# The mLSTM's running maximum spread over the partitions and masked by GpSimd instead of by TensorE products

## The chip, the core and the metric

One NeuronCore of a Trainium2 chip runs the whole program in one launch. The metric is device time in microseconds (us), the median over executions. PE is TensorE, ACT ScalarE, DVE VectorE, POOL GpSimd, SP the queue that issues the weight loads.

## What is computed

Two layers, each an FFN, a mixing sub-layer of three branches (stick-breaking attention, mLSTM, latent attention) and another FFN, over 256 tokens of width 1024. The change lies in the mLSTM branch: four heads of 128, chunks of 128, started from a zero state. Per head:

```python
cum_f = jnp.einsum('bhs,ts->bht', lfc, lower_incl)
log_intra = jnp.where(causal, cum_f[..., :, None] - cum_f[..., None, :] + igc[..., None, :], -jnp.inf)
log_inter = cum_f + m_prev[..., None]
m = jnp.maximum(log_inter, jnp.max(log_intra, axis=-1))
w_intra = jnp.exp(log_intra - m[..., None])
scores = jnp.einsum('bhtd,bhsd->bhts', qc, kc) * w_intra
num = scores @ vc + w_inter[..., None] * (qc @ c_prev)
h_out = num / jnp.maximum(jnp.abs(den), jnp.exp(-m))[..., None]
```

The kernel treats both chunks at once. With g = ig - cum and mx the running maximum of g (not below 0), the weight of key s for query t is exp(g[s] - mx[t]) for s <= t, otherwise 0. Keys lie on the partitions, so g is a bias per partition, while mx, a row over the queries, has to be spread over all 128 partitions.

## The kernel before

The program is written out ahead of time by a planner in the kernel itself. The main line is a list of units, each some TensorE products with a weight tile; weights come from memory as fp32 (`raw`), ScalarE rounds them to a high part (`whi`, or `g` where a larger buffer is used), VectorE subtracts to get the low part (`wlo<-raw,whi`, a subtraction of two SBUF tiles of 128x1024), and three products make one of full precision. All else (norms, attention heads, mLSTM heads) runs as side work: Python generators that name, at each `yield`, the engine they go to next, the tiles they read and the buffers they need. Between units the planner lets every side go on whose inputs it reckons ready by costs of its own (`Flow.cost`, which charges a POOL instruction other than tensor_tensor 60 ns and 0.8 ns a column), and so fixes the order of each engine's queue. Each engine then runs its queue strictly in that order, and waits where an input isn't there.

The mLSTM is in two of these. `ml_side` transposes the gates to rows, scans them to `cum` and `mx`, and lays the gate columns `gcol` out by partitions. It had each row twice (8 rows), to hold mx as a high and a low part in a tile `mv` (tag R3). `ml_head`, once per head, spread mx with a product of the constant `sel` and `mv` into PSUM (`pd`), added the mask with two bf16 products, and took the scores in another (`pS`). Then ScalarE's exponential with bias g, VectorE's multiply with the scores, TensorE's product with the values (129 columns: the last one sums), and a normalisation: squares on ScalarE, six small vector instructions, a reciprocal root on POOL (`rstd`: an add and a power), and two output rows `xn` on VectorE. `y_t` transposes the output for two heads at a time.

In names of the profile and of the order, digits behind a letter are left out: `t` is the scratch tag t384 with six buffers (t_2 is t384_2), `at` a PSUM bank, `R` one of R1 (convolved q and k), R3 or R4, `consts_bf` the bf16 identity and masks, `qk` the stick-breaking pair's q and k. All instructions of the helpers carry the helper's line, L213 before and L210 in the changed kernel, so they are told by tiles.

Of the kernel before, what the change touches and what calls it, by code (L numbers as in the profile page):

```python
# [24 lines left out]
BIG = 1e30  # L25
# [4 lines left out]
NSMALL = GATES - MLI  # L30
R_SB, R_ML, R_GATE, R_CONVW, R_CONVB, R_QN, R_KVN, R_G1, R_G2, R_G3, N_ROWS = (
    0, 4, 12, 36, 68, 76, 78, 79, 87, 95, 103)
C_ID, C_TRI, C_ONES, C_INVF, C_MSB, C_MML, C_MLA, C_SEL, C_ROW, C_END = (
    0, 128, 256, 384, 416, 544, 672, 800, 1312, 1316)

LN128 = float(np.float32(128.0 ** -0.5))
RS128 = float(np.float32(128.0 ** -0.5))
# [4 lines left out]
def host_consts():  # L42
    c = np.zeros((P, C_END), np.float32)
    i = np.arange(P)
    row, col = i[:, None], i[None, :]
    c[:, C_ID:C_ID + P] = np.eye(P, dtype=np.float32)
    c[:, C_TRI:C_TRI + P] = np.where(row >= col, -1.0, 0.0)
    c[:, C_ONES:C_ONES + P] = -1.0
    c[:, C_MSB:C_MSB + P] = np.where(row >= col, -BIG, 0.0)
    c[:, C_MML:C_MML + P] = np.where(row > col, BIG, 0.0)  # L50
    c[:, C_MLA:C_MLA + P] = np.where(col > row, -BIG, 0.0)
    f = np.power(np.float32(10000.0), -np.arange(16, dtype=np.float32) / np.float32(16)).astype(np.float32)
    c[:, C_INVF:C_INVF + 16] = f
    c[:, C_INVF + 16:C_INVF + 32] = f
    for h in range(4):
        c[[h, h + 4], C_SEL + h * P:C_SEL + (h + 1) * P] = 1.0
    c[0:8, C_ROW:C_END] = [[1, 0, float(r >= 4), 1 - 2 * float(r >= 4)] for r in range(8)]
    return c


# [166 lines left out]
class Trunk:  # L227
# [248 lines left out]
    def setup(self, N):  # L476
        nc, a = self.nc, self.a
        self.c = self.const([P, C_MSB], "consts")
        self.xg = self.const([P, 8 + 8 * S], "x")
        self.x = self.xg[:, 8:].rearrange("p (k c) -> p k c", k=8)  # L480
        self.sel = self.const([P, 4, P], "sel", F32R)
        self.ident = self.c[:, C_ID:C_ID + P]
        self.tri = self.const([P, P], "tri", F32R)
        self.nones = self.c[:, C_ONES:C_ONES + P]
        self.ones_r = self.const([P, P], "ones_r", F32R)
        self.cb = self.const([P, 4, P], "consts_bf", BF16)
        self.ident_bf = self.cb[:, 0, :]
        self.mask_sb, self.mask_ml, self.mask_mla = (self.cb[:, i, :] for i in (1, 2, 3))
        self.mhalf = self.const([P, 16], "mhalf")
        self.row = self.const([8, 4], "row")  # L490
# [46 lines left out]
    def setup_late(self):  # L537
        nc, a = self.nc, self.a
        nc.sync.dma_start(self.c[:, C_TRI:C_ONES], a["consts"][:, C_TRI:C_ONES])
        nc.sync.dma_start(self.c[:, C_INVF:], a["consts"][:, C_INVF:C_MSB])  # L540
        sel = self.sb([P, 4, P], "qk96", 2)
        nc.sync.dma_start(sel, a["consts"][:, C_SEL:C_ROW].rearrange("p (h c) -> p h c", h=4))
        nc.sync.dma_start(self.row, a["consts"][0:8, C_ROW:C_END])
        msk = self.t384([P, 3, P])
        nc.sync.dma_start(msk, a["consts"][:, C_MSB:C_SEL].rearrange("p (m c) -> p m c", m=3))
# [5 lines left out]
        nc.vector.tensor_copy(self.cb[:, 1:4, :], msk)  # L551
        self.give(msk)
        nc.vector.tensor_copy(self.sel, sel)
        nc.vector.tensor_copy(self.tri, self.c[:, C_TRI:C_TRI + P])
        posf = self.sb([P, 2], "posf")
        nc.vector.tensor_copy(posf, pos)
# [27 lines left out]
        m = 1.5 * 2.0 ** 23  # L584
# [389 lines left out]
    def plan_mix(self, l, U, M, N):  # L974
        nc, a = self.nc, self.a
# [8 lines left out]
        def first_side():  # L984
            yield lambda: "row" in U,
            M["small"] = self.sb([P, 2, NSMALL], "small")
            M["sbv"] = self.sb([P, 2, 256], "sbv")
            M["ifg"] = self.sb([P, 2, 2, 2, 4], "ifg")
            M["done"] = set()
            M["mla"] = {}  # L990
            for t in range(2):
                yield "v", box[0][:, t], U["r"]
                r = U["r"][:, t:t + 1]
                nc.vector.scalar_tensor_tensor(M["small"][:, t], box[0][:, t, :NSMALL], r, M["bias1"][:, :NSMALL], ALU.mult, ALU.add)
                nc.vector.tensor_copy(M["ifg"][:, t], M["small"][:, t, 0:8].rearrange("p (g h) -> p g h", g=2).unsqueeze(2).to_broadcast([P, 2, 2, 4]))
# [423 lines left out]
    def ml_side(self, M):  # L1419
        nc = self.nc  # L1420
        small = M["small"]
        gates = M["ifg"].rearrange("p t g d h -> p t g (d h)")
        yield "p", small, ("ps", 1), (lambda: self.exp_ready(M))
        pt = self.ps()
        for t in range(2):
            for g in range(2):
                nc.tensor.transpose(pt[0:8, g * S + t * P:g * S + (t + 1) * P], gates[:, t, g], self.ident)
        rows = self.sb([8, 3, S], "R4")
        e, cum, g = rows[:, 0], rows[:, 1], rows[:, 2]
        mv = self.sb([P, S + P], "R3", dt=F32R)  # L1430
# [7 lines left out]
        nc.vector.scalar_tensor_tensor(e, pt[0:8, S:], 0.0, e, ALU.min, ALU.subtract)  # L1438
        nc.vector.tensor_tensor_scan(cum, one.to_broadcast([8, S]), e, 0.0, ALU.mult, ALU.add)
        nc.vector.tensor_tensor(g, pt[0:8, :S], cum, ALU.subtract)  # L1440
        self.give(pt)
        yield "v",
        mx, e = e, cum
        nc.vector.tensor_tensor_scan(mx, zero.to_broadcast([8, S]), g, 0.0, ALU.add, ALU.max)
        nc.vector.tensor_tensor(e, cum, mx, ALU.add)
        yield "a", e
        nc.scalar.activation(e, e, AF.Exp, scale=-1.0)

        nc.vector.tensor_copy(mv[0:8, 0:S], mx)
        nc.vector.tensor_scalar(mx, mx, low, None, ALU.mult)  # L1450
        nc.vector.scalar_tensor_tensor(mv[0:8, 0:S], mv[0:8, 0:S].bitcast(F32), sign, mx, ALU.mult, ALU.add)
        nc.vector.tensor_copy(mv[0:8, S:], mv[0:8, P:S].bitcast(F32))
        yield "p", e, ("ps", 1)
        pc = self.ps()
        for t in range(2):
# [14 lines left out]
    def ml_head(self, h, M, B):  # L1470
# [1 line left out]
        mm = nc.tensor.matmul  # L1472
        mx, gc, y = B["mx"], B["gc"], B["y"]
        qk, v, og = M["mlqk"], M["mlv"], M["og"]
        yield "p", mx, ("ps", 2), ("t384", 1)
        pd, pS, w = self.ps(), self.ps(), self.t384()
        mm(pd[:, 0:384], lhsT=self.sel[:, h, :], rhs=mx, start=True, stop=False, skip_group_check=True)
        for o in (0, 256):
            mm(pd[:, o:o + 128], lhsT=self.ident_bf, rhs=self.mask_ml, start=False, stop=True, skip_group_check=True)
        mm(pS[:, 0:256], lhsT=qk[:, 4 + h, 0:128], rhs=qk[:, h, :], start=True, stop=True)  # L1480
        mm(pS[:, 256:384], lhsT=qk[:, 4 + h, 128:256], rhs=qk[:, h, 128:256], start=True, stop=True)
        yield "a", pd[:, :384]
        for s, sl in ((0, slice(0, 256)), (1, slice(256, 384))):
# [110 lines left out]
```

## Time and profile before

| | |
|---|---|
| Time, median of 3 (lowest to highest) | 810.89 us (810.3 to 811.42) |
| Profiled execution, its time | 811.12 us |
| Its span | 809.1 us |
| Mean granted TensorE clock | 0.999 of full |
| TensorE busy | 801.9 us (99%) |
| VectorE, ScalarE busy | 611.8 us (76%), 472.3 us (58%) |
| POOL busy | 33.2 us (4%), 50 instructions |

The span runs from the first to the last instruction; the time also holds some 2 us around it. TensorE's busy time counts products that overlap, so lengths of steps are read from start to start. Busy shares say where the work is; what a change is worth shows in who waits for whom.

### The profile page before, as it was taken

Reading aid. Unit: us, or ns where it says so; the run is one execution under the profiler, and the core shown is the slowest. Engines: PE = TensorE matmul, PEld = TensorE weight load, DVE = VectorE, ACT = ScalarE, POOL = GpSimd, SP = SyncE. Lnnn points to the kernel's source line nnn. Section 1 sums busy time; section 2 is a strip of 40 time slices with the busy share of each in tenths; the row PEclk is TensorE's granted clock in tenths of the full one; section 3 lists DMA queues with packets and bytes.
Section 4 is the critical chain, followed back from the end, with each engine's and each line's share of the span. In section 5 each row is a group of like instructions: output and inputs, shape, how many; then the busy total and the mean of one; then the engine's idle time right before and its main releaser. Section 6 shows DMA issues by size and latency. Waiting matters only on the chain.

```text
span 809.1 us, 14902 instructions
## 1 busy us (share of the span) xinstructions
PE 801.9 (99%) x5927; PEld 756.6 (94%) x5927; DVE 611.8 (76%) x1023; ACT 472.3 (58%) x776; POOL 33.2 (4%) x50
## 2 busy tenths in 40 slices
PE   8999999999999999999999999999999999999998
PEld 6999999899999999889988899998999999988887
DVE  4888878987766588986787768789977585888851
ACT  5656545657686546765556555565567845657530
POOL 0000001200200000000000000110002000000000
PEclk9999999999999999999999999999999999999999
DMA  8767744653344745775576656266553555476721
GB/s 260 235 199 252 254 131 122 220 176 116 105 153 162 254 164 199 238 239 184 152 233 206 182 170 195 74 191 187 157 158 98 180 187 188 160 223 220 236 73 52
DMA packets 43844, 145.30 MB, mean 180 GB/s; under 512 B 6016, under 2 KB 7296, under 8 KB 43776
## 3 DMA queue, kind: packets, MB, share of 16 engines
q1 hardware_dynamic: 43632, 144.10, 56.3%
q8 instruction: 46, 0.75, 0.4%
q10 hardware_dynamic: 144, 0.27, 0.1%
q14 instruction: 22, 0.18, 0.1%
HBM read 143.30 MB, written 1.05 MB: 178 GB/s over the span
## 4 chain that ended last, share of the span: by engine, by line
PE 97%; DMA 1%; DVE 0%; ACT 0%; SPq 0%; issue 0%; ACTq 0%; DVEq 0%
PE mm L213 66%; PE at L213 31%; DMA raw<-in_weights_dram 1%; SPq L213 0%; DVE t L213 0%; ACT g L213 0%; DVE hs L213 0%; ACT s2k L213 0%; DVE g L213 0%; DVE u L213 0%; DVE xn L213 0%; ACT u L213 0%; ACTq L213 0%; DVEq L213 0%
## 5 line engine op out<-in xcount | busy, mean ns | idle before, releaser
L213 PE MATMUL mm<-u,whi 128*128 128x256 f32 (+1 forms) x1432 | 299.4, 300 | 0.0
L213 ACT CAST whi<-raw 128x1024 fp32r<-128x1024 f32 (+3 forms) x184 | 187.9, 1032 | 132.5 <-DMA raw<-in_weights_dram 54.9
L213 DVE TENSOR_TENSOR wlo<-raw,whi 128x1024 fp32r<-128x1024 f32 (+3 forms) x184 | 218.1, 1195 | 43.2 <-ACT whi L213 42.4
L213 PEld LDWEIGHTS mm<-u,whi 128*128 128x128 f32 x1432 | 227.1, 188 | 10.8 <-issue 0.5
L213 PE MATMUL mm<-u,wlo 128*128 128x256 f32 x840 | 234.2, 279 | 0.0
L213 PE MATMUL mm<-u,g 128*128 128x512 f32 (+1 forms) x992 | 156.5, 316 | 2.5 <-ACT g L213 2.1
L213 PEld LDWEIGHTS mm<-u,wlo 128*128 128x128 f32 x840 | 157.7, 188 | 0.0
L213 PEld LDWEIGHTS mm<-u,g 128*128 128x128 f32 x992 | 139.4, 192 | 15.5 <-ACT g L213 3.0
L213 ACT CAST g<-raw 128x1024 fp32r<-128x1024 f32 (+3 forms) x89 | 90.0, 1014 | 76.1 <-DMA raw<-in_weights_dram 45.3
L213 DVE TENSOR_TENSOR g<-raw,g 128x1024 fp32r<-128x1024 f32 (+3 forms) x89 | 104.2, 1178 | 13.0 <-ACT g L213 12.7
L213 PE MATMUL at<-R,whi 128*128 128x256 f32 x416 | 73.4, 278 | 0.0
L213 PE MATMUL at<-R,g 128*128 128x256 f32 x552 | 66.4, 279 | 0.0
L213 PEld LDWEIGHTS at<-R,g 128*128 128x128 f32 x552 | 65.2, 188 | 0.0
L213 PEld LDWEIGHTS at<-R,whi 128*128 128x128 f32 x416 | 63.3, 187 | 0.1
L213 PE MATMUL at<-R,wlo 128*128 128x256 f32 x208 | 57.8, 278 | 0.0
L213 PE MATMUL mm<-whi,u 128*128 128x512 f32 (+1 forms) x168 | 55.0, 384 | 0.0
L213 PEld LDWEIGHTS at<-R,wlo 128*128 128x128 f32 x208 | 39.0, 187 | 0.0
L213 DVE TENSOR_TENSOR R<-s2k,R 128x256 fp32r<-128x256 f32 (+1 forms) x39 | 17.9, 458 | 26.3 <-ACT R L213 26.0
L213 PEld LDWEIGHTS mm<-whi,u 128*128 128x128 f32 x168 | 31.6, 188 | 5.0
L213 PE MATMUL mm<-wlo,u 128*128 128x512 f32 (+1 forms) x84 | 32.1, 382 | 0.0
L213 DVE TENSOR_TENSOR s2k<-s2k,mm 128x512 f32<-128x512 f32 x38 | 26.0, 683 | 2.9 <-ACT s2k L213 2.5
L213 POOL TENSOR_TENSOR rcol<-rcol,mhalf 128x2 f32<-128x2 f32 x6 | 7.8, 1298 | 488.2 <-DVE rcol L213 488.2
(214 smaller groups left out, 984.8 us busy)
## 6 DMA issues: line engine op xcount, KB each, us to landing
raw<-in_weights_dram SPq DMA_DIRECT2D x245, 512.0 KB, 4.3
raw<-in_weights_dram SPq DMA_DIRECT2D x14, 384.0 KB, 3.5
raw<-in_weights_dram SPq DMA_DIRECT2D x8, 424.0 KB, 3.6
raw<-in_weights_dram SPq DMA_DIRECT2D x6, 256.0 KB, 4.5
bc<-in_b_in_dram SPq DMA_DIRECT2D x2, 512.0 KB, 4.6
x<-in_x_dram SPq DMA_DIRECT2D x3, 256.0 KB, 6.5
out_dram<-xn SPq DMA_DIRECT2D x3, 256.0 KB, 2.1
mg<-in_ml_out_norm_dram SPq DMA_DIRECT2D x2, 256.0 KB, 4.9
```

What stands on the lines that cost most here:

```text
L213: f(*args, **kw)
```

## The change

The row mx is no longer spread and masked by TensorE. Four small copies through SP put the four rows at partitions 0, 32, 64 and 96 of `mv`. In each head POOL spreads its row over 128 partitions (`partition_broadcast`) into the scratch tile `w`; ScalarE takes the exponential there, and POOL then sets the entries above the diagonal to zero (`affine_select`, twice per head). The constants `sel` and the mask of the mLSTM, the doubled rows and the instructions that made the hi and lo parts go.

```diff
@@ setup_late, plan_mix (first_side)
-        sel = self.sb([P, 4, P], "qk96", 2)
-        nc.sync.dma_start(sel, a["consts"][:, C_SEL:C_ROW].rearrange("p (h c) -> p h c", h=4))
...
-        nc.vector.tensor_copy(self.sel, sel)
...
-                nc.vector.tensor_copy(M["ifg"][:, t], M["small"][:, t, 0:8].rearrange("p (g h) -> p g h", g=2).unsqueeze(2).to_broadcast([P, 2, 2, 4]))
+                nc.vector.tensor_copy(M["ifg"][:, t], M["small"][:, t, 0:8].rearrange("p (g h) -> p g h", g=2))
@@ ml_side
-        mv = self.sb([P, S + P], "R3", dt=F32R)
-        nc.gpsimd.memset(mv.bitcast(F32), 0.0)
...
-        nc.vector.tensor_copy(mv[0:8, 0:S], mx)
-        nc.vector.tensor_scalar(mx, mx, low, None, ALU.mult)
-        nc.vector.scalar_tensor_tensor(mv[0:8, 0:S], mv[0:8, 0:S].bitcast(F32), sign, mx, ALU.mult, ALU.add)
-        nc.vector.tensor_copy(mv[0:8, S:], mv[0:8, P:S].bitcast(F32))
+        mv = self.sb([P, S], "R3")
+        for h in range(4):
+            nc.sync.dma_start(mv[32 * h:32 * h + 1], mx[h:h + 1])
@@ ml_head
-        yield "p", mx, ("ps", 2), ("t384", 1)
-        pd, pS, w = self.ps(), self.ps(), self.t384()
-        mm(pd[:, 0:384], lhsT=self.sel[:, h, :], rhs=mx, start=True, stop=False, skip_group_check=True)
-        for o in (0, 256):
-            mm(pd[:, o:o + 128], lhsT=self.ident_bf, rhs=self.mask_ml, start=False, stop=True, skip_group_check=True)
+        yield "g", mx, ("t384", 1)
+        w = self.t384()
+        nc.gpsimd.partition_broadcast(w[:, 0:256], mx[32 * h:32 * h + 1])
+        yield "p", w[:, 0:256], ("ps", 1)
+        pS = self.ps()
         mm(pS[:, 0:256], lhsT=qk[:, 4 + h, 0:128], rhs=qk[:, h, :], start=True, stop=True)
         mm(pS[:, 256:384], lhsT=qk[:, 4 + h, 128:256], rhs=qk[:, h, 128:256], start=True, stop=True)
-        yield "a", pd[:, :384]
-        for s, sl in ((0, slice(0, 256)), (1, slice(256, 384))):
-            nc.scalar.activation(w[:, sl], pd[:, sl], AF.Exp, bias=gc[:, 0, s, h:h + 1], scale=-1.0)
-        self.give(pd)
+        yield "a", w[:, 0:256]
+        for s, o, sl in ((1, 256, slice(128, 256)), (0, 0, slice(0, 256))):
+            nc.scalar.activation(w[:, o:384 if s else 256], w[:, sl], AF.Exp, bias=gc[:, 0, s, h:h + 1], scale=-1.0)
+
+        yield "g", w
+        for o in (0, 256):
+            nc.gpsimd.affine_select(w[:, o:o + P], w[:, o:o + P], [[1, P]], ALU.is_ge, 0.0, 0, -1)
         yield "v", w
```

Since the planner sets the order by its costs, instructions move. First place, the queue of POOL around the heads of the first layer. Before, from the last reciprocal root of the latent attention on:

```order
L213 TENSOR_TENSOR rstd_305_1935<-rstd_305_1935,mhalf_92 128x8
L213 MEMSET mlv_2078 128x8x2
L213 MEMSET R_352_2255 128x384
L213 TENSOR_SCALAR rstd_417_2589<-hs_2561 128x2
L213 TENSOR_TENSOR rstd_417_2589<-rstd_417_2589,mhalf_92 128x2
```


Now the memset of `R` has gone, and the heads' work stands there. An ISA row without a tile is a reload of POOL's code library, which the build puts in ahead of the broadcasts (ISA rows with tiles) and again ahead of the add and power of the roots:

```order
L210 MEMSET mlv_2074 128x8x2
L210 ISA
L210 ISA t_2_417_2639<-R_387_2475 128x256
L210 ISA t_4_419_2650<-R_387_2475 128x256
L210 ISA t_3_421_2660<-R_387_2475 128x256
L210 ISA t_5_422_2662<-R_387_2475 128x256
L210 AFFINE_SELECT t_2_417_2639<-t_2_417_2639 128x128 x2
L210 AFFINE_SELECT t_4_419_2650<-t_4_419_2650 128x128 x2
L210 AFFINE_SELECT t_3_421_2660<-t_3_421_2660 128x128 x2
L210 AFFINE_SELECT t_5_422_2662<-t_5_422_2662 128x128 x2
L210 ISA
L210 TENSOR_SCALAR rstd_438_2736<-hs_2695 128x2
```


All four broadcasts now stand ahead of all selects, and the second reload between the last select and the first root.

Second place, the queue of TensorE in the second layer. Before, the first head's spreading and scores stood in the middle of the first stick-breaking pair (its identity and triangle products `consts`, `tri`), and its product with the values soon after:

```order
L213 MATMUL at_1107_7158<-t_3_1113_7164,tri_89 128x384
L213 MATMUL at_1123_7267<-R_1078_6966,sel_88 128x384
L213 LDWEIGHTS consts_bf_91
L213 MATMUL at_1123_7267<-consts_bf_91 128x128
L213 LDWEIGHTS consts_bf_91
L213 MATMUL at_1123_7267<-consts_bf_91 128x128
L213 MATMUL at_1124_7268<-R_974_6315 128x256
L213 MATMUL at_1124_7268<-R_974_6315 128x128
L213 MATMUL at_1108_7159<-t_2_1110_7161,consts_86 128x128
L213 MATMUL at_1108_7159<-t_4_1112_7163,tri_89 128x384
L213 MATMUL at_1108_7159<-t_5_1114_7165,tri_89 128x384
L213 MATMUL mm_1094_7090<-u_5758,whi_7076 128x256 x2
```


Now the pair comes first. Behind its last triangle product (`t_5`, `tri`) and the scores of head 0, and ahead of the first head's product with the values (`mlv`), stand head 1's scores, six weight products and the pair's outputs:

```order
L210 MATMUL at_1125_7290<-R_968_6306 128x256
L210 MATMUL at_1125_7290<-R_968_6306 128x128
L210 MATMUL mm_1087_7079<-u_5749,whi_7065 128x256 x2
L210 MATMUL mm_1087_7079<-u_5749,wlo_7066 128x256
L210 MATMUL mm_1087_7079<-u_5749,whi_7065 128x256 x2
L210 MATMUL mm_1087_7079<-u_5749,wlo_7066 128x256
L210 MATMUL at_1127_7309<-t_0_1101_7150,sbv_6129 64x256
L210 MATMUL at_1127_7309<-t_1_1102_7151,sbv_6129 64x256
L210 MATMUL at_1127_7309<-t_0_1101_7150,sbv_6129 64x128
L210 MATMUL at_1127_7309<-t_1_1102_7151,sbv_6129 64x128
L210 MATMUL at_1128_7314<-mlv_6715,t_2_1117_7257 128x129 x3
```


The heads' value products come after the pair now, since their tiles t_2 to t_5 are those that the triangle products of the pair read. In the first layer the same stands with three heads' scores and no weight products between, and with all four heads' value products in a row after the outputs, then 60 weight products and the transposes of the heads' output.

Third place, the second layer's POOL and VectorE. On POOL the reload and the root of head 0 have come ahead of the selects of head 3 (t_5):

```order
L210 AFFINE_SELECT t_2_1117_7257<-t_2_1117_7257 128x128 x2
L210 AFFINE_SELECT t_4_1121_7271<-t_4_1121_7271 128x128 x2
L210 AFFINE_SELECT t_3_1123_7281<-t_3_1123_7281 128x128 x2
L210 ISA
L210 TENSOR_SCALAR rstd_1135_7342<-hs_7318 128x2
L210 TENSOR_TENSOR rstd_1135_7342<-rstd_1135_7342,mhalf_91 128x2
L210 AFFINE_SELECT t_5_1124_7283<-t_5_1124_7283 128x128 x2
L210 TENSOR_SCALAR rstd_1142_7385<-hs_7323 128x2
```


On VectorE, from the multiply of head 0 (t_2) on, a weight subtraction stands between the multiplies of head 0 and 1:

```order
L210 SCALAR_TENSOR_TENSOR t_2_1117_7257<-at_1120_7268,t_2_1117_7257 128x384
L210 TENSOR_TENSOR wlo_7244<-raw_7101,whi_7243 128x1024
L210 SCALAR_TENSOR_TENSOR t_4_1121_7271<-at_1122_7278,t_4_1121_7271 128x384
L210 TENSOR_TENSOR g_6_1049_6855<-at_1127_7309,g_6_1049_6855 128x256
L210 COPY hs_7318<-at_1128_7314 128x2
```


Further on in the same queue the multiply of head 3 (t_5) stands behind head 0's use of its root (`hs<-hs,rstd`), behind the reload that is:

```order
L210 TENSOR_TENSOR hs_7323<-hs_7323 128x2
L210 SCALAR_TENSOR_TENSOR hs_7318<-hs_7318,rstd_1135_7342 128x2
L210 SCALAR_TENSOR_TENSOR xn_7172<-at_1128_7314,hs_7318,xn_6591 128x128 x2
L210 SCALAR_TENSOR_TENSOR hs_7323<-hs_7323 128x2
L210 SCALAR_TENSOR_TENSOR t_5_1124_7283<-at_1134_7338,t_5_1124_7283 128x384
L210 COPY hs_7380<-at_1140_7376 128x2
```


So in this layer head 3's weights are masked and multiplied only after a library reload and a root; before, head 3's multiply also stood behind head 0's root on VectorE, but no reload and no masking on POOL came ahead of it.

## Rows read from the trace of the kernel before

**Rows 1.** The page's parts 1 and 4: busy time, and the chain's shares.
```profile
PE 801.9 (99%) x5927; PEld 756.6 (94%) x5927; DVE 611.8 (76%) x1023; ACT 472.3 (58%) x776; POOL 33.2 (4%) x50
...
PE 97%; DMA 1%; DVE 0%; ACT 0%; SPq 0%; issue 0%; ACTq 0%; DVEq 0%
```

**Rows 2.** Waits of TensorE, whole span: total us, times, longest.
```profile
PE mm L213 <- ACT g L213: 2.1, 1, 2.1
...
PE at L213 <- DVE t L213: 0.2, 1, 0.2
```

**Rows 3.** Timeline of TensorE, second layer's heads: start, us, engine, line, operation.
```profile
606.21 0.34 PE L213 MATMUL at<-R,sel 128*128 128x384 f32 x1
...
606.51 0.87 PE L213 MATMUL at<-R 128*128 128x256 f32 x4
607.22 0.39 PE L213 MATMUL at<-t,consts 128*128 128x128 f32 x2
607.36 0.60 PE L213 MATMUL at<-t,tri 128*128 128x384 f32 x2
...
608.50 0.83 PE L213 MATMUL at<-mlv,t 128*128 128x129 f32 x6
609.08 0.42 PE L213 MATMUL at<-R,sel 128*128 128x384 f32 x1
...
609.46 0.87 PE L213 MATMUL at<-R 128*128 128x256 f32 x4
610.26 0.87 PE L213 MATMUL at<-t,sbv 128*64 128x256 f32 x8
611.07 0.44 PE L213 MATMUL at<-R,sel 128*128 128x384 f32 x1
```

**Rows 4.** Timeline of TensorE, first layer: three weight products from start to start.
```profile
207.24 0.28 PE L213 MATMUL mm<-u,wlo 128*128 128x256 f32 x1
...
207.59 0.28 PE L213 MATMUL mm<-u,wlo 128*128 128x256 f32 x1
```

**Rows 5.** Groups of POOL by form: busy us, mean ns, idle before.
```profile
L213 POOL TENSOR_TENSOR rstd<-rstd,mhalf 128x8 f32<-128x8 f32 x4 | 6.9, 1722 | 0.3
...
L213 POOL MEMSET R<- 128x384 f32 x2 | 0.8, 419 | 0.0
...
L213 POOL MEMSET mlv<- 128x16 f32 x2 | 0.2, 112 | 0.0
```

**Rows 6.** Timeline of POOL, second layer's last two heads.
```profile
618.30 0.22 POOL L213 TENSOR_SCALAR rstd<-hs 128x2 f32<-128x2 f32 x1 [1.10 <-DVE hs L213]
618.61 0.72 POOL L213 TENSOR_TENSOR rstd<-rstd,mhalf 128x2 f32<-128x2 f32 x1
621.61 1.13 POOL L213 TENSOR_SCALAR rstd<-hs 128x2 f32<-128x2 f32 x1 [2.29 <-DVE hs L213]
622.82 1.55 POOL L213 TENSOR_TENSOR rstd<-rstd,mhalf 128x2 f32<-128x2 f32 x1
```

**Rows 7.** Timeline of VectorE, second layer's heads.
```profile
610.08 0.16 DVE L213 COPY hs<-at 128x2 f32<-128x2 f32 x1 [0.86 <-ACT s2k L213]
...
611.14 0.56 DVE L213 SCALAR_TENSOR_TENSOR t<-at,t 128x384 f32<-128x384 f32 x1
...
612.57 0.61 DVE L213 SCALAR_TENSOR_TENSOR xn<-at,hs,xn 128x128 f32<-128x128 f32 x2
...
621.44 2.35 DVE L213 TENSOR_TENSOR wlo<-raw,whi 128x1024 fp32r<-128x1024 f32 x2
```

**Rows 8.** Timeline of POOL at the start.
```profile
0.97 0.11 POOL L213 MEMSET mhalf<- 128x16 f32 x1
26.01 1.54 POOL L213 TENSOR_TENSOR rcol<-rcol,mhalf 128x2 f32<-128x2 f32 x1 [24.93 <-DVE rcol L213]
```

**Rows 9.** DMA issues: count, KB each, median us to landing.
```profile
raw<-in_weights_dram SPq DMA_DIRECT2D x245, 512.0 KB, 4.3
...
consts<-in_consts_dram SPq DMA_DIRECT2D x1, 16.0 KB, 5.2
```

More of the change, by code (lines that the diff above doesn't have):

```diff
@@ L32 @@
     0, 4, 12, 36, 68, 76, 78, 79, 87, 95, 103)
-C_ID, C_TRI, C_ONES, C_INVF, C_MSB, C_MML, C_MLA, C_SEL, C_ROW, C_END = (
-    0, 128, 256, 384, 416, 544, 672, 800, 1312, 1316)
+C_ID, C_TRI, C_ONES, C_INVF, C_MSB, C_MLA, C_ROW, C_END = (
+    0, 128, 256, 384, 416, 544, 672, 674)
 LN128 = float(np.float32(128.0 ** -0.5))
@@ L49, in host_consts @@
     c[:, C_MSB:C_MSB + P] = np.where(row >= col, -BIG, 0.0)
-    c[:, C_MML:C_MML + P] = np.where(row > col, BIG, 0.0)
     c[:, C_MLA:C_MLA + P] = np.where(col > row, -BIG, 0.0)
@@ L54, in host_consts @@
     c[:, C_INVF + 16:C_INVF + 32] = f
-    for h in range(4):
-        c[[h, h + 4], C_SEL + h * P:C_SEL + (h + 1) * P] = 1.0
-    c[0:8, C_ROW:C_END] = [[1, 0, float(r >= 4), 1 - 2 * float(r >= 4)] for r in range(8)]
+    c[:, C_ROW:C_END] = 1, 0
     return c
@@ L480, in setup @@
         self.x = self.xg[:, 8:].rearrange("p (k c) -> p k c", k=8)
-        self.sel = self.const([P, 4, P], "sel", F32R)
         self.ident = self.c[:, C_ID:C_ID + P]
@@ L485, in setup @@
         self.ones_r = self.const([P, P], "ones_r", F32R)
-        self.cb = self.const([P, 4, P], "consts_bf", BF16)
+        self.cb = self.const([P, 3, P], "consts_bf", BF16)
         self.ident_bf = self.cb[:, 0, :]
-        self.mask_sb, self.mask_ml, self.mask_mla = (self.cb[:, i, :] for i in (1, 2, 3))
+        self.mask_sb, self.mask_mla = (self.cb[:, i, :] for i in (1, 2))
         self.mhalf = self.const([P, 16], "mhalf")
-        self.row = self.const([8, 4], "row")
+        self.row = self.const([4, 2], "row")
         self.cs = self.const([P, 2, 2, 32], "cossin")
@@ L540, in setup_late @@
         nc.sync.dma_start(self.c[:, C_INVF:], a["consts"][:, C_INVF:C_MSB])
-        sel = self.sb([P, 4, P], "qk96", 2)
-        nc.sync.dma_start(sel, a["consts"][:, C_SEL:C_ROW].rearrange("p (h c) -> p h c", h=4))
-        nc.sync.dma_start(self.row, a["consts"][0:8, C_ROW:C_END])
-        msk = self.t384([P, 3, P])
-        nc.sync.dma_start(msk, a["consts"][:, C_MSB:C_SEL].rearrange("p (m c) -> p m c", m=3))
+        nc.sync.dma_start(self.row, a["consts"][0:4, C_ROW:C_END])
+        msk = self.t384([P, 2, P])
+        nc.sync.dma_start(msk, a["consts"][:, C_MSB:C_ROW].rearrange("p (m c) -> p m c", m=2))
         pos = self.sb([P, 2], "pos", dt=I32)
@@ L550, in setup_late @@
         nc.vector.tensor_copy(self.cb[:, 0, :], self.ident)
-        nc.vector.tensor_copy(self.cb[:, 1:4, :], msk)
+        nc.vector.tensor_copy(self.cb[:, 1:3, :], msk)
         self.give(msk)
-        nc.vector.tensor_copy(self.sel, sel)
         nc.vector.tensor_copy(self.tri, self.c[:, C_TRI:C_TRI + P])
@@ L987, in first_side @@
             M["sbv"] = self.sb([P, 2, 256], "sbv")
-            M["ifg"] = self.sb([P, 2, 2, 2, 4], "ifg")
+            M["ifg"] = self.sb([P, 2, 2, 4], "ifg")
             M["done"] = set()
@@ L1421, in ml_side @@
         small = M["small"]
-        gates = M["ifg"].rearrange("p t g d h -> p t g (d h)")
+        gates = M["ifg"]
         yield "p", small, ("ps", 1), (lambda: self.exp_ready(M))
@@ L1426, in ml_side @@
             for g in range(2):
-                nc.tensor.transpose(pt[0:8, g * S + t * P:g * S + (t + 1) * P], gates[:, t, g], self.ident)
-        rows = self.sb([8, 3, S], "R4")
+                nc.tensor.transpose(pt[0:4, g * S + t * P:g * S + (t + 1) * P], gates[:, t, g], self.ident)
+        rows = self.sb([4, 3, S], "R4")
         e, cum, g = rows[:, 0], rows[:, 1], rows[:, 2]
-        mv = self.sb([P, S + P], "R3", dt=F32R)
-        nc.gpsimd.memset(mv.bitcast(F32), 0.0)
-        one, zero, low, sign = (self.row[:, i:i + 1] for i in range(4))
-        yield "a", pt[0:8]
-        nc.scalar.activation(e, pt[0:8, S:], AF.Abs)
+        one, zero = (self.row[:, i:i + 1] for i in range(2))
+        yield "a", pt[0:4]
+        nc.scalar.activation(e, pt[0:4, S:], AF.Abs)
         nc.scalar.activation(e, e, AF.Exp, scale=-1.0)
@@ L1437, in ml_side @@
         yield "v", e
-        nc.vector.scalar_tensor_tensor(e, pt[0:8, S:], 0.0, e, ALU.min, ALU.subtract)
-        nc.vector.tensor_tensor_scan(cum, one.to_broadcast([8, S]), e, 0.0, ALU.mult, ALU.add)
-        nc.vector.tensor_tensor(g, pt[0:8, :S], cum, ALU.subtract)
+        nc.vector.scalar_tensor_tensor(e, pt[0:4, S:], 0.0, e, ALU.min, ALU.subtract)
+        nc.vector.tensor_tensor_scan(cum, one.to_broadcast([4, S]), e, 0.0, ALU.mult, ALU.add)
+        nc.vector.tensor_tensor(g, pt[0:4, :S], cum, ALU.subtract)
         self.give(pt)
@@ L1443, in ml_side @@
         mx, e = e, cum
-        nc.vector.tensor_tensor_scan(mx, zero.to_broadcast([8, S]), g, 0.0, ALU.add, ALU.max)
+        nc.vector.tensor_tensor_scan(mx, zero.to_broadcast([4, S]), g, 0.0, ALU.add, ALU.max)
         nc.vector.tensor_tensor(e, cum, mx, ALU.add)
```

## The prediction, on record before the changed kernel ran

> **What bounds the kernel now.** I read the page's first and fourth part, then who waited for whom on TensorE, then the two stretches in which the mLSTM heads run. TensorE is busy 801.9 of 809.1 us and is 97% of the chain that ended last [rows 1]. It waits for another engine hardly at all: 2.1 us at the start, and in both mLSTM stretches together once, 0.2 us [rows 2]. So whatever leaves TensorE is gained in full, and whatever makes its queue wait is lost in full, because the queue is in order: behind a waiting product stand weight products that could have run. POOL, which gets the work, is almost idle, and that is no argument: what counts is when its results are there.
>
> **What TensorE saves.** In one head the product with `sel` starts at 606.21 and the scores after the two mask products at 606.51, so 0.30 us; in the next 609.08 to 609.46, 0.38 [rows 3]. Of the eight heads two show 0.30, one 0.40 and five 0.38 (for one of these, with a wait inside, I take 0.38): **2.9 us saved**. The vector work that built the hi/lo rows, the copy of `sel` and one memset go too; those engines were not waited for, so I cost that at nothing.
>
> **What POOL has to do, and when.** The order of the changed program decides this. The heads now come after the first stick-breaking pair, whose tiles t384_2 to t384_5 they reuse. Per layer POOL runs four broadcasts, eight selects, and a library reload on either side. The first reload stands behind the `mlv` memset, tens of us ahead of the heads, and I take it as covered. The four row copies on SP are issued before that pair starts on TensorE, more than fifty weight products of 0.117 us [rows 4] ahead of the first broadcast: 6 us, against landings of 4.3 to 5.2 us [rows 9]. Covered as well; without the cover, broadcasts would start up to 5 us later. SP is past that point anyway, since the weight load ahead of the copies waits for a later vector instruction than the scan that they read.
>
> Prices. A broadcast p of 128x256 isn't in the trace. A memset writes 0.42 us for 384 columns and 0.11 for 16, so 0.84 ns a column [rows 5]; a small POOL instruction takes 0.22 [rows 6]; reading and writing 256 columns gives 0.22+2x0.21 = 0.65 from below. From above the dearest POOL row, 1.72 us for powers of 8 columns [rows 5]. Between them 1.2: one row has to reach 128 partitions, which no row of POOL here does, so I stay away from the lower end. A select s of 128x128: 0.22 from below, 0.72 (the two-column power, [rows 6]) from above; 0.22+0.11 = 0.33, I take 0.35, as one streaming input is nearest to the memset. A trap beside it: POOL's 0.22 becomes 1.13 and its 0.72 becomes 1.55 where a vector subtraction of two SBUF tiles (1.2 us each) is running [rows 6, 7].
>
> The reload, L. In this trace one reload stands between the memset of `mhalf` and the next POOL instruction 24.9 us later [rows 8], which waited for VectorE: L is between 0 and 24.9. If the code comes in as any transfer does (that is assumed), transfers of 16 and 512 KB land after 5.2 and 4.3 us [rows 9] give an estimate of 5.
>
> The Trainium skill (GPSIMD Engine Reference, 2.1 Instruction dispatch) says that the first call into freshly loaded code costs about 6 us (5.95 measured) that no instruction in a profile shows. No run here shows it yet; by it the sum below would be 2 x 0.95 = 1.9 us more.
>
> **First layer.** T is the end of the pair's last triangle product. Products on the way: scores 0.71 (606.51 to 607.22), the pair's identity and triangle products 0.58, six weight products 0.70 (together 607.22 to 608.50), pair outputs 0.81 (610.26 to 611.07), a head's value products 0.58 (608.50 to 609.08) [rows 3, 4]. The first two broadcasts may start 2.2 us before T, when the triangle products of the pair's first head are done (one of them 0.22, six weight products, one scores, and the other head's 0.58 follow), the last two only near T, since their tiles are read there. So the broadcasts end at E = T + max(0.1+2p, 4p-2.1) = T+2.7, and the selects follow all of them. Head 0 is ready after two selects, the vector multiply of 0.56 [rows 7] and two handovers of 0.05: T+2.7+0.7+0.66 = T+4.06. TensorE has three scores, 2.1 us, and then stands: **2.0 us**. The other heads come every 0.7 us, TensorE needs 0.58 plus the pair outputs, so no more is lost there.
>
> Then the way back. The reload starts when the selects end, T+5.5; the reciprocal roots of all heads are behind it. At T+10.5 come POOL's add and power (1.03, [rows 6]), a small vector instruction and two output rows (0.77, [rows 7]), and for head 1 the same again with the power held up by a subtraction (to T+14.45), then 0.8: T+15.3. TensorE ended the heads at T+7.2 and has 60 weight products, 7.0 us, until it transposes: T+14.2. **1.1 us** lost; with L below 3.9, nothing.
>
> **Second layer.** Same start, but TensorE has 2.9 us (two scores, six weight products, outputs): **1.15**. VectorE has a subtraction between the multiplies of head 0 and 1, so head 1 comes 1.7 us after head 0 while TensorE needs 0.58: **1.1**. That subtraction also holds the third head's selects, which end at T+5.9. Here the reload stands before the selects of head 3, and VectorE too has head 0's root ahead of head 3's multiply. Reload to 10.9, add and power to 11.95, selects to 12.65, multiply to 13.4; TensorE arrives at 11.1 (after 12 and 18 weight products): **2.3**, and nothing with L below 2.7. The last transposes then wait for POOL and two subtractions, as they nearly do now: **0.6**.
>
> Sum: 2.0+1.1+1.15+1.1+2.3+0.6 = 8.25 lost, 2.9 saved, +5.35. The profiled execution took 811.12 us (0.2 over the median of 810.89), so **816.5 us**.
>
> **Rivals.**
> *All of it hides (faster).* Place: the heads' first wait. With p=0.65, s=0.22 and L under 2.7, E is T+1.4, head 0 ready at T+2.5, 0.4 lost in layer one and 0.7 in layer two: 1.1 against 2.9, -1.8, **809.3**. POOL's short rows speak for it, the work that crosses partitions against. It turns at lost = 2.9: with L hidden, p about 0.9.
> *The reload is in the background, the rest as taken.* Lost 4.85: +2, **813.1**. For it: nothing else uses POOL meanwhile; against: the roots stand right behind.
> *The load is paid at the first use.* Then the early reload covers nothing, the first broadcast in each layer comes 5 us later and nothing behind it is spared: 10 more, **826.5**. For it: nothing in the rows says when the code comes in; against: after the reload at the start, the first power, 24.9 us later, took 1.54 [rows 8], no longer than the 1.55 of one late in the kernel [rows 6]. The page of the Trainium skill quoted above could be read so.
> *Broadcasts are far dearer.* At p=3, E is T+9.9, 7.2 more in each layer: **831**. For it: no row shows any work across partitions on POOL; against: POOL's two-column rows are short.
>
> That the products stay is excluded: the order has none with `sel`.
>
> **How the numbers follow.** The forecast case (813.5 to 822 by s up to 0.72, p 0.8 to 1.7, L 3 to 8) 0.47; background reload 0.15; first use 0.12; dear broadcasts 0.17; all hidden 0.09. A measurement of this kernel tells about 0.2% (1.6 us) from no change: faster 0.07, same 0.10 (edges of the hidden and background cases), slower 0.83. For 8 in 10 the range leaves out most of the hidden case below and half of the dear case above: 810.5 to 830; the forecast's own is 813.5 to 822.
>
> **What would show it.** TensorE's waits in the two stretches, now 0.2 us, become about 8 us, on VectorE by name (the multiply, the output rows), with POOL behind it in VectorE's own waits. POOL's start-to-start distance gives p and s; the gap between the last select ahead of the reload and the first add, longer than its input's lateness, gives L. Wrong would be: TensorE without waits there (POOL hides), a gap in front of the first broadcast (first use), or waits elsewhere, for instance on weights held up by ScalarE's exponentials that queue behind the broadcasts.

## The result and the profile after

The changed kernel takes 817.09 us (815.99 to 819.27), the kernel before 811.15 in the same rounds: 1.0072 of it, interval 1.0053 to 1.0092, so 5.9 us slower. Forecast were 816.5, with a range of 813.5 to 822. The profiled execution took 816.89, its span is 815.2. Parts 1 and 4 of its page, to be held against [rows 1]:

```profile
PE 801.3 (98%) x5903; PEld 756.3 (93%) x5903; DVE 607.7 (75%) x1014; ACT 473.4 (58%) x776; POOL 41.6 (5%) x72
...
PE 95%; DMA 1%; issue 1%; DVE 1%; POOL 0%; ACT 0%; SPq 0%; DVEq 0%; ACTq 0%
```

TensorE is busy 0.6 us less (its busy time also holds products run at a lower clock, see below) and its span is 6.1 us longer, so it now stands still. Who it waited for, over the whole span (us in total, times, longest), against [rows 2]:

```profile
PE at L210 <- DVE t L210: 4.4, 1, 4.4
PE mm L210 <- DVE u L210: 2.7, 1, 2.7
PE at L210 <- DVE xn L210: 2.1, 1, 2.1
PE mm L210 <- POOL mhalf L210: 1.1, 1, 1.1
```

The second and fourth rows lie in the start of the program, where before had such waits too (2.1, 1.1 and 0.3). New are 4.4 us for a `t`, a head's multiply, and 2.1 us for `xn`, a head's output. POOL's timeline (start, us, operation, idle before and what ended it) shows where both come from. First layer:

```profile
208.59 0.98 POOL L210 PARTITION_BROADCAST t<-R  x2 [54.61 <-DVE t L210]
210.46 0.96 POOL L210 PARTITION_BROADCAST t<-R  x2 [0.89 <-PE at L210]
211.49 1.64 POOL L210 TENSOR_SCALAR_AFFINE_SELECT t<-t 128x128 f32<-128x128 f32 x6
213.43 0.54 POOL L210 TENSOR_SCALAR_AFFINE_SELECT t<-t 128x128 f32<-128x128 f32 x2 [0.29 <-ACT t L210]
221.05 0.24 POOL L210 TENSOR_SCALAR rstd<-hs 128x2 f32<-128x2 f32 x1 [7.09 <-issue]
221.38 0.74 POOL L210 TENSOR_TENSOR rstd<-rstd,mhalf 128x2 f32<-128x2 f32 x1
223.12 1.26 POOL L210 TENSOR_SCALAR rstd<-hs 128x2 f32<-128x2 f32 x1 [0.99 <-DVE hs L210]
```

Second layer:

```profile
607.86 0.98 POOL L210 PARTITION_BROADCAST t<-R  x2 [58.64 <-DVE t L210]
609.73 0.96 POOL L210 PARTITION_BROADCAST t<-R  x2 [0.89 <-PE at L210]
610.77 2.67 POOL L210 TENSOR_SCALAR_AFFINE_SELECT t<-t 128x128 f32<-128x128 f32 x6
621.18 0.24 POOL L210 TENSOR_SCALAR rstd<-hs 128x2 f32<-128x2 f32 x1 [7.74 <-issue]
621.50 0.74 POOL L210 TENSOR_TENSOR rstd<-rstd,mhalf 128x2 f32<-128x2 f32 x1
622.22 0.55 POOL L210 TENSOR_SCALAR_AFFINE_SELECT t<-t 128x128 f32<-128x128 f32 x2
```

Two broadcasts take 0.98 us together, six selects 1.64. Both are short. In the second layer the six take 2.67, since one of them, here taken alone, ran while VectorE subtracted a weight:

```profile
611.88 1.32 POOL L210 TENSOR_SCALAR_AFFINE_SELECT t<-t 128x128 f32<-128x128 f32 x1
611.83 1.22 DVE L210 TENSOR_TENSOR wlo<-raw,whi 128x1024 fp32r<-128x1024 f32 x1
```

The add at 223.12 in the first layer, 1.26 us where others take 0.22 to 0.24, met such a subtraction too. Between the last select ahead of the reload and the first root lie 7.1 us in layer 1 (213.97 to 221.05) and 7.7 us in layer 2, put down to "issue", POOL waiting for nothing that the trace shows. The root's input was there long before: VectorE, second layer:

```profile
615.52 0.15 DVE L210 SCALAR_TENSOR_TENSOR hs<-hs 128x2 f32<-128x2 f32 x1
...
622.28 0.24 DVE L210 SCALAR_TENSOR_TENSOR hs<-hs,rstd 128x2 f32<-128x2 f32 x1 [5.75 <-POOL rstd L210]
...
623.15 0.55 DVE L210 SCALAR_TENSOR_TENSOR t<-at,t 128x384 f32<-128x384 f32 x1
```

Head 0's input, `hs`, was done at 615.7 (the first row). VectorE goes on with head 1 until 616.5 and then stands until the root is back, and head 3's multiply (623.15) comes behind it, as its selects on POOL (622.22) stand behind the reload as well. On TensorE, the second transposes of the first layer, and head 3's value products with the first weight products behind them:

```profile
223.29 0.38 PE L210 MATMUL at<-consts,xn 128*128 128x128 f32 x2
225.81 0.59 PE L210 MATMUL at<-consts,xn 128*128 128x128 f32 x2 [2.15 <-DVE xn L210]
...
623.76 1.45 PE L210 MATMUL at<-mlv,t 128*128 128x129 f32 x6 [4.42 <-DVE t L210]
624.86 0.78 PE L210 MATMUL mm<-u,whi 128*128 128x256 f32 x2
```

And by stretch in the second layer (length, then busy us of PE, PEld, DVE, ACT, POOL; granted clock; DMA):

```profile
600.00:619.00 19.00, 18.93 (x161) 17.94 (x158) 8.39 (x22) 15.78 (x40) 4.55 (x10) 1.00 0.37 113
619.00:623.70 4.70, 0.34 (x3) 0.13 (x2) 1.39 (x6) 0.00 (x0) 1.80 (x6) 1.00 0.00 0
623.70:627.60 3.90, 3.84 (x18) 3.72 (x18) 2.98 (x20) 0.63 (x4) 1.56 (x3) 0.56 0.00 0
627.60:640.00 12.40, 12.40 (x111) 11.82 (x111) 9.74 (x15) 10.44 (x20) 2.66 (x2) 1.00 0.48 138
```

In the stretch behind the 4.4 us in which TensorE stood, the granted clock is 0.56, nearly the lower of its two levels (1.2 GHz); ahead of it and from 627.6 on it is 1.00. The 12 weight products at 624.86 took 2.74 us, where 12 at full clock take 1.40, and head 3's six value products 1.10 in place of 0.59 for those of the head before it: 1.85 us more. Behind the 2.1 us of the first layer the windows show 1.00.

Added up start to start over all rows of TensorE in the two stretches, the products with `sel` and the masks were worth 3.0 us. So some 9.1 us (6.1 + 3.0) were lost, of which the two waits make 6.5 and the lower clock 1.85. Of the rest 0.3 us are longer waits at the start; some 0.4 stay without a name. The drawn-out add of the first layer is part of its 2.1 us: VectorE stood another 0.9 us for that head's root, so about that much of the 2.1 (an estimate) comes on top of the reload.

### The profile page after: what moved, and what is told of

It is laid out like the page before. It is cut to its first block, busy times and chain, and to the rows that moved or that the text cites. A ratio compares the mean times of both kernels' runs of the same rounds, so it can differ in the third digit from the quotient of the medians.

```text
span 815.2 us, 14888 instructions
## 1 busy us (share of the span) xinstructions
PE 801.3 (98%) x5903; PEld 756.3 (93%) x5903; DVE 607.7 (75%) x1014; ACT 473.4 (58%) x776; POOL 41.6 (5%) x72
## 4 chain that ended last, share of the span: by engine, by line
PE 95%; DMA 1%; issue 1%; DVE 1%; POOL 0%; ACT 0%; SPq 0%; DVEq 0%; ACTq 0%
PE mm L210 65%; PE at L210 30%; DMA raw<-in_weights_dram 1%; POOL rstd L210 0%; DVE hs L210 0%; ACT s2k L210 0%; DVE xn L210 0%; SPq L210 0%; ACT g L210 0%; DVE g L210 0%; DVE t L210 0%; DVE u L210 0%; ACT u L210 0%; ACT whi L210 0%; DVEq L210 0%
## 5 line engine op out<-in xcount | busy, mean ns | idle before, releaser
L210 PE MATMUL mm<-u,whi 128*128 128x256 f32 (+1 forms) x1448 | 303.4, 300 | 0.0
L210 ACT CAST whi<-raw 128x1024 fp32r<-128x1024 f32 (+2 forms) x185 | 188.7, 1030 | 135.2 <-DMA raw<-in_weights_dram 49.0
L210 DVE TENSOR_TENSOR wlo<-raw,whi 128x1024 fp32r<-128x1024 f32 (+2 forms) x185 | 218.8, 1194 | 41.7 <-ACT whi L210 41.2
L210 PEld LDWEIGHTS mm<-u,whi 128*128 128x128 f32 x1448 | 230.3, 188 | 10.8 <-issue 0.5
L210 PE MATMUL mm<-u,wlo 128*128 128x256 f32 x848 | 236.8, 279 | 0.0
L210 PE MATMUL mm<-u,g 128*128 128x512 f32 (+1 forms) x968 | 153.5, 317 | 2.9 <-DVE u L210 2.7
L210 PEld LDWEIGHTS mm<-u,g 128*128 128x128 f32 x968 | 136.5, 192 | 15.8 <-ACT g L210 3.6
L210 ACT CAST g<-raw 128x1024 fp32r<-128x1024 f32 (+2 forms) x88 | 89.1, 1016 | 78.9 <-DMA raw<-in_weights_dram 44.1
L210 DVE TENSOR_TENSOR g<-raw,g 128x1024 fp32r<-128x1024 f32 (+2 forms) x88 | 103.0, 1180 | 13.9 <-ACT g L210 11.2
L210 PE MATMUL at<-R,g 128*128 128x256 f32 x534 | 64.1, 279 | 0.0
```

Of the source, the lines that this page charges most:

```text
L210: f(*args, **kw)
```

## The experiments

**Theory A.** A reload of POOL's code occupies POOL for 6.5 to 7.7 us whenever it is executed, and costs TensorE what stands behind it on POOL and is due. **Theory B.** It is paid by the first instruction that uses the new code. **Theory C.** It isn't the reload but the new order and the hand-overs between POOL, VectorE and TensorE. **Theory D.** A reload disturbs the rest of the chip.

**Reloads added.** To the changed kernel, ahead of the first root of each layer, so that three reloads stand there in place of the build's one (`_reserved_1` is the other library):

```diff
+        if "lib" not in B:
+            B["lib"] = True
+            self.tc.nc.gpsimd.load_library(library_config.standard)
+            self.tc.nc.gpsimd.load_library(library_config._reserved_1)
+            self.tc.nc.gpsimd.load_library(library_config.standard)
         r = self.rstd(s[:, 3, :], 2)
```

> In each layer two more reloads of POOL's code (the standard library, the other one, the standard one) stand in a row between the last select and the first root of the heads; nothing else is changed. Theory A, the reload itself blocks POOL's queue for about 7.4 us each time it is executed (the gaps of 7.1 and 7.7 us in the changed kernel): the roots come about 15 us later in each layer, TensorE's wait at the transposes of layer 1 grows from 2.1 to about 17 us and that of head 3 in layer 2 from 4.4 to about 19 us, in all +29 us and something for the lower clock behind such waits: 846 to 850 us. Theory B, the load is paid by the first instruction that needs the new code: three reloads in a row cost as much as one, 817 us. Theory C, the gap ahead of the roots is no cost of the reload but of the order of the queues (the hand-overs between POOL, VectorE and TensorE): 817 us, and no longer gap on POOL.

Measured 845.99 us (1.0429 of before, 1.0413 to 1.0444), at the lower edge of what A gave. POOL at the two places, and TensorE's waits:

```profile
212.91 0.54 POOL L210 TENSOR_SCALAR_AFFINE_SELECT t<-t 128x128 f32<-128x128 f32 x2 [0.29 <-ACT t L210]
233.61 0.24 POOL L210 TENSOR_SCALAR rstd<-hs 128x2 f32<-128x2 f32 x1 [20.16 <-issue]
...
625.12 2.67 POOL L210 TENSOR_SCALAR_AFFINE_SELECT t<-t 128x128 f32<-128x128 f32 x6
649.04 0.24 POOL L210 TENSOR_SCALAR rstd<-hs 128x2 f32<-128x2 f32 x1 [21.24 <-issue]
```

```profile
PE at L210 <- DVE t L210: 17.9, 1, 17.9
PE at L210 <- DVE hs L210: 12.7, 1, 12.7
```

The gap grew from 7.1 to 20.2 and from 7.7 to 21.2 us: three reloads, 6.7 and 7.1 us each on average, with no instruction between them that could use the code. That excludes B, and C for the gap itself. TensorE's wait for head 3 is 17.9 us, as A has it; in layer 1 12.7 us fell on an earlier step of VectorE's (`hs`) and 2.0 on `xn`.

**Reloads in the kernel before, at two places.** The same pair of reloads, once in `ml_side` ahead of the memset of `mv` (named `R` in the rows), where POOL is idle, once in `ml_head` behind the first head's root:

```diff
+        self.tc.nc.gpsimd.load_library(library_config._reserved_1)
+        self.tc.nc.gpsimd.load_library(library_config.standard)
```

> The kernel before, with two reloads of POOL's code (the other library, then the standard one) added in each layer right behind the mlv memset, where POOL stands idle for some 50 us; every other instruction stays where it was. Theory A, a reload costs only what waits behind it on POOL: 810.5 to 812 us, no change. Theory D, a reload disturbs the rest of the chip too (its transfer, or something that stops other engines): two or more us slower.

> The same two reloads in each layer, but behind the first head's root, so that the roots of heads 1 to 3 stand behind them. Theory A: some 13.4 us of POOL; the root of head 1 comes 12 us later in layer 1 and 9.6 in layer 2, VectorE's queue stands behind it with the next subtractions of weights, and TensorE waits 6 to 9 us in each layer, with a stretch at half clock behind it: 824 to 832 us. Theory B, paid once by the first use: 813 to 818 us. With the run beside it the pair says whether it is the place or the reload that costs.

Measured 811.82 us (1.0002, 0.9992 to 1.0012) and 833.52 us (1.027, 1.0255 to 1.0286). POOL in the first (both layers), then in the second, then TensorE's waits in the second:

```profile
169.18 0.41 POOL L213 MEMSET R<- 128x384 f32 x1 [13.60 <-issue]
...
563.41 0.41 POOL L213 MEMSET R<- 128x384 f32 x1 [13.80 <-issue]
```

```profile
222.01 0.24 POOL L213 TENSOR_SCALAR rstd<-hs 128x2 f32<-128x2 f32 x1 [13.49 <-issue]
...
637.23 0.24 POOL L213 TENSOR_SCALAR rstd<-hs 128x2 f32<-128x2 f32 x1 [13.10 <-issue]
```

```profile
PE at L213 <- DVE xn L213: 8.0, 1, 8.0
PE at L213 <- DVE hs L213: 7.9, 1, 7.9
```

The pair takes 13.1 to 13.8 us at either place, whether a memset or an add stands behind it. Where nothing is due it costs nothing, which excludes D; ahead of three roots it costs 22 us, somewhat over the 13 to 21 expected: two waits of 8 us, and the granted clock is 0.53 to 0.87 in the windows of 8 and 10 us around them. How the 22 us divide between the waits and the lower clock was not worked out.

**Roots elsewhere.** In the changed kernel:

```diff
-        r = self.rstd(s[:, 3, :], 2)
+        r = self.sb([P, 2], "rstd2", bufs=8)
+        nc.vector.tensor_scalar(r, s[:, 3, :], EPS, None, ALU.add)
+        yield "a", r
+        nc.scalar.activation(r, r, AF.Ln)
+        nc.scalar.activation(r, r, AF.Exp, scale=-0.5)
         yield "v", r
```

> The heads' reciprocal roots leave POOL: a small add on VectorE, then ScalarE's logarithm and exponential. Broadcasts and selects stay, and the reload back falls ahead of the next root on POOL, about 100 us later. Theory A, the reload is what costs: the waits of 2.1 us (transposes, layer 1) and 4.4 us (head 3, layer 2) go, and with them the stretch at half clock behind the second; of 9.1 us lost against before (5.9 slower with 3.2 us of products saved) some 8.5 go: 808 to 809.5 us. Theory C, the order of the heads behind the stick-breaking pair and POOL's hand-overs in front of the exponential and the multiply cost: these stay as they are, 814 us or more.

Measured 806.69 us, 0.9942 of before (0.9926 to 0.9959), better than A's range by 1.3 us. TensorE's waits, complete:

```profile
PE mm L210 <- ACT g L210: 2.3, 1, 2.3
PE mm L210 <- POOL mhalf L210: 1.1, 1, 1.1
```

Both are those of the program's start. Broadcasts, selects and the order of the heads behind the pair are as in the changed kernel; only the reload is no longer in anybody's way (the next root on POOL comes 102 to 106 us later). So the order of the heads and the hand-overs of broadcasts and selects are not what costs, and the change with its reload out of the way is a gain of some 4.6 us (3.3 to 6.0 by the interval). The products that went make 3.0 of it and the one wait of before 0.2; the rest isn't found by name. That the roots' own place on POOL costs is still open here; the control and the run with transfers below bear on it.

The control:

> A control: the kernel before with nothing but the roots of the heads moved off POOL, as in the run with the roots elsewhere. If the gain there comes from the products that went and the reload that no longer blocks the roots (theory A), this one gains nothing by itself: 810.3 to 812 us. If it comes from the roots themselves being faster off POOL (rival), it gains here too: 807.5 to 809.5 us.

Measured 811.72 us (0.9997, 0.9984 to 1.0011). By itself the move gains nothing. Its outputs are wrong, by a cause that stays open, so I take this only as a hint; the run with transfers below leaves the roots on POOL and gains all the same.

**All roots behind all selects.**

```diff
+        B["s"] = B.get("s", 0) + 1
...
-        yield "v", s
+        yield "v", s, (lambda: B["s"] == 4)
```

> A condition of the planner holds every root until the selects of all four heads have been given out, so that in layer 2 head 3's selects no longer stand behind the reload; layer 1 has that order already. Theory A: in layer 2 the wait of 4.4 us for head 3 and the half clock behind it (some 1.7 us) go, while the reload now delays only the roots; the transposes then wait up to as long as in layer 1 (2.1 us): 811 to 813.5 us. Theory C (hand-overs and order, not the reload): within 1 us of 817.

Measured 819.52 us (1.0103, 1.0079 to 1.0127): neither theory's range holds it. POOL in the second layer, and TensorE's longest wait:

```profile
616.86 0.55 POOL L210 TENSOR_SCALAR_AFFINE_SELECT t<-t 128x128 f32<-128x128 f32 x2 [2.62 <-ACT t L210]
624.46 0.24 POOL L210 TENSOR_SCALAR rstd<-hs 128x2 f32<-128x2 f32 x1 [7.04 <-issue]
```

```profile
PE at L210 <- DVE xn L210: 7.7, 3, 4.9
```

Head 3's scores come late, so its selects do (616.86), and the reload starts only behind them, at 617.4, 8.7 us after the first broadcast, where in the changed kernel it is 5.6. It lasts 7.0 us as ever, and now all four heads' outputs wait for it: in layer 2 TensorE waits 4.9 and 0.5 us for them, where it had waited 4.4 for head 3, and the granted clock behind that is 0.53 for 7.2 us (0.56 for 3.9 before). Layer 1, whose order is the same as in the changed kernel, waits 2.25 us at its transposes, for 2.15 there, yet here the clock falls behind the wait:

```profile
225.30:229.40 4.10, 4.05 (x26) 3.48 (x27) 3.74 (x10) 0.97 (x2) 1.44 (x3) 0.58 0.36 130
```

The loss agrees with theory A, read from the trace after the miss; what I had left out is that a condition that moves work ahead of a reload moves the reload back.

**Selects alone**, spreading by products as before (the kernel before, with its two mask products and no others replaced):

> The kernel before, with the row still spread by the products with sel, but masked by the selects on POOL in place of the bf16 mask products. No broadcast, so no reload stands in the program behind the first one. Theory A: the mask products (0.5 us in layer 1, 0.8 in layer 2 by the two traces) are saved and 0.27 us selects are hidden or nearly: 809.5 to 811.5 us. Theory C, the extra hop through POOL inside each head costs: 813 us or more.

Measured 811.34 us (0.9996, 0.9987 to 1.0005). That is within A's range: no reload and no loss, but no gain either. In its profile, taken of one of its slower executions (812.26 us), TensorE's waits at the start are 1.9 us longer and 0.5 us of small ones are new in the heads; that this is where the 1.3 us of mask products went is argued, not shown.

**The reload early, and no reload.** Three ways to spread into tiles of their own, so that exponentials don't have to wait for the pair's tiles. On POOL with the reload back written at once:

```diff
+        yield "g", mv
+        for h in range(4):
+            nc.gpsimd.partition_broadcast(own[h], mv[32 * h:32 * h + 1])
+        self.tc.nc.gpsimd.load_library(library_config.standard)
```

by transfers through memory:

```diff
-        for h in range(4):
-            nc.sync.dma_start(mv[32 * h:32 * h + 1], mx[h:h + 1])
+        nc.sync.dma_start(self.rowd, mx)
+        for h in range(4):
+            nc.sync.dma_start(mv[h], self.rowd[h].partition_broadcast(P))
```

and by VectorE:

```diff
+        for h in range(4):
+            for o in range(0, P, 32):
+                nc.sync.dma_start(mv[h][o:o + 1], mx[h:h + 1])
...
+        nc.vector.stream_shuffle(mx, mx, [0] * 32)
```

> All four broadcasts go as one step, into tiles of their own, as soon as the rows have landed, and the reload of the standard library is written straight behind them; the exponentials read from those tiles, selects and roots stay on POOL. So the reload stays in the program, 6.5 to 7.7 us long by the gaps measured, but runs while the stick-breaking pair is still on TensorE. Theory A, a reload costs only what is queued behind it on POOL and is due: some 0 to 2 us may be left where the first selects come right behind it: 807 to 810 us. Theory C, a reload or the hand-overs through POOL cost by themselves, wherever they stand: 812 us or more.

> The rows go to memory in one transfer and come back spread over the 128 partitions in four (128 KB each), into tiles of their own; no broadcast on POOL and so no reload behind the start. Selects and roots stay on POOL. Theory A: 806.5 to 809 us, as with the roots elsewhere, since the selects were hidden there too; if the two transfers (some 2 to 5 us each by the landings in the trace) are later than the planner reckons, up to 2 us more. Theory C, selects and roots on POOL cost by themselves: 811 us or more.

> Each row is copied to the partitions 0, 32, 64 and 96 of a tile of its own (16 small transfers) and spread there by VectorE's shuffle within each 32 partitions, in place; two memsets on POOL clear the tiles first. No broadcast, no reload. Selects and roots stay on POOL. Theory A: 806.5 to 809.5 us, VectorE being given four small instructions in exchange for those that made the hi and lo rows. Theory C: 811 us or more.

Measured 811.15 us (0.9989, 0.9977 to 1.0), 808.1 us (0.9955, 0.9938 to 0.9971) and 811.14 us (0.9987, 0.9975 to 1.0). The second is as A has it. The first is between the two ranges, and the third lies where C put it, so both have to be explained. POOL of the first in layer 1, and TensorE's wait for the heads' multiplies:

```profile
202.59 0.96 POOL L210 PARTITION_BROADCAST mv<-R  x2
211.17 1.03 POOL L210 TENSOR_SCALAR_AFFINE_SELECT t<-t 128x128 f32<-128x128 f32 x4 [7.62 <-ACT t L210]
```

```profile
PE at L210 <- DVE t L210: 2.8, 3, 1.3
```

The broadcasts end at 203.5, the first select starts at 211.17, although ScalarE's exponentials for it, which the row names, were done by about 209.4: the reload had nearly six us of cover and wanted 7.6. What it lacked, TensorE waited: 1.2 and 1.3 us at the two first heads, 2.8 us in all. The run with transfers has the same structure and no reload; it has 0.2 us of that wait and is 3.05 us faster, and as its selects and roots are on POOL, those cost little by themselves: its interval overlaps that of the run with the roots elsewhere. For the third the trace gives a reason of its own, on VectorE in layer 1:

```profile
209.33 0.01 DVE L210 LOAD_MASK_SELECT mv<-mv  x1 [2.10 <-DMA mv<-R]
209.35 0.45 DVE L210 STREAM_SHUFFLE mv<-mv 128x256 f32<-128x256 f32 x1
209.69 0.63 DVE L210 TENSOR_TENSOR t<-t,t 128x384 fp32r<-128x384 f32 x1
```

The last of 16 small transfers lands at 209.3; the shuffle that waits for it, 2.1 us, holds up the pair's own instruction behind it, and TensorE waits 2.2 us for ScalarE's step of the pair (`t`) behind it. That this is the whole of the 3 us it lost on the run with transfers is argued; no run takes it away.

**Both remedies, and the broadcasts kept without the early reload:**

> The two remedies together: rows spread by transfers through memory, roots on VectorE and ScalarE; only the selects are left on POOL. Theory A (the reload was all that the change lost, 8.5 us, and each remedy removes it): nothing is left to gain over the better of the two, 806 to 808 us.

> Broadcasts on POOL into tiles of their own as soon as the rows have landed, no reload behind them by hand, roots on VectorE and ScalarE, selects on POOL. The reload back falls ahead of the next root on POOL, about 100 us later. In the run with the reload written straight behind the broadcasts TensorE waited 1.2 and 1.3 us for the first multiply, since the first selects stood behind the reload; theory A: these go, 806 to 808 us. Rival: they are the hand-overs through POOL, and stay: 809 to 811 us.

Measured 807.4 us (0.9946, 0.9929 to 0.9963) and 806.89 us (0.9944, 0.9929 to 0.9959). As A has it: the two remedies don't add, since they remove the same loss, and the waits at the first multiplies are gone once no reload stands ahead of the selects. The best here, 0.9942 to 0.9946 of the kernel before with the roots off POOL, can't be told apart, with POOL's broadcasts or without.

## Why the prediction was right

The time came out as forecast, 816.5 against 817.09, and the signs named were there: TensorE waits for a multiply and for output rows, with POOL behind them. But the forecast named two causes, and only the smaller held. Work queued behind the reload, 3.4 of its 8.25 us, is what the runs show; the heads' first waits, 4.25 us, put down to slow broadcasts and to a subtraction between two multiplies, did not come. That the total fits all the same is luck: the errors cancel.

- **Saved:** 2.9 us forecast, 3.0 measured.
- **The broadcast p:** taken at 1.2, between 0.65 and 1.72; measured 0.49, below the lower end. The step that failed is "I stay away from the lower end": work across partitions was assumed to be dear, with no row for it. The select s, 0.35, measured 0.27.
- **So the heads' first waits are not there:** 2.0 us in layer 1, 1.15 and 1.1 in layer 2, 4.25 of the 8.25 us; TensorE's waits show none of them, and start to start head 1 of layer 2 came some 0.2 us late. (The 2.0 was mis-summed as well: in layer 1 the pair's outputs, 0.81 us, stand ahead of the value products, so by the forecast's own numbers 1.2 were lost there and 1.9 at the transposes; the sum is the same.) The formula held: with p = 0.49 the last broadcast should end at T+1.1 (T, the end of the last triangle product, is 210.38); it ended at 211.42.
- **The reload L:** taken at 5; the gaps are 7.1 and 7.7 us, and 6.5 to 7.1 on average for several in a row. The selects ended at T+3.6 in place of T+5.5, the reload at T+10.7 in place of T+10.5: here the two errors cancel. The last transposes of the pair started at 225.81, T+15.4, against T+15.3.
- **Transposes in layer 1:** 1.1 forecast, 2.1 measured, as TensorE came earlier: it was there at T+12.9 in place of T+14.2, having waited for no head. The forecast had the power of the second head's root held up by a subtraction of VectorE's; held up was its add, to 1.26 us. **Head 3 in layer 2:** 2.3 forecast, 4.4 measured, since TensorE was again early and the reload long, and 1.85 us of lower clock behind it, a term that the sum did not have. The last 0.6 was 0.
- **The sum:** 8.25 lost forecast, 6.5 + 1.85 = 8.35 found by name of 9.1. The reload's two waits were sized at about half (3.4 for 6.5), the heads' first waits at 4.25 for next to nothing.

Of the rivals, the background reload is excluded by the gaps, the payment at first use by three reloads in a row, the dear broadcast by its row. "All of it hides" would have been right for the broadcasts and selects, as the run with the roots elsewhere shows; it was the reload alone that decided the sign. The Trainium skill (GPSIMD Engine Reference, 2.1 Instruction dispatch) has about 6 us, 5.95 measured, for the first call into loaded code. The gaps here are 7.1 and 7.7 us for single reloads; and they stand at the reload, used or not, and whatever follows: three in a row cost 20.2 and 21.2 us, and in the idle run it was a memset that waited.

## What to carry to other kernels

A change of GpSimd's code library is an instruction of some 7 us that no line of this kernel's source shows: list where the build puts it, in each queue's order, and ask what is behind it and due. A move to an idle engine is judged by the instructions on either side of the moved ones; here broadcasts and selects were nearly free, and what they did to the next root made a gain of 0.6% into a loss of 0.7%. And where a change makes TensorE wait, read the granted clock of the stretch behind the wait as well: behind the 4.4 us here the lower clock cost another 1.85.

## What was not expected of the hardware

A broadcast of one row of 256 fp32 over 128 partitions took 0.49 us on GpSimd (two in 0.98), less than one power of two columns (0.74); VectorE's shuffle within 32 partitions took 0.45. A wait of 4.4 us was followed by 3.9 us at a granted clock of 0.56, one of 2.15 us by none that the windows show, and one of 2.25 us in another run by 4.1 us at 0.58: these runs give no length of wait from which the clock falls. A select of 0.27 us and an add of 0.24 took 1.32 and 1.26 while VectorE ran a subtraction of two SBUF tiles. Two reloads in a row cost 13.1 to 13.8 us, and where POOL was idle the time did not show them.
